# A hybrid decoder layer on one core: output weights of the second token group parted anew by add transfers, and another order of the last half-group

## The chip, the core and the metric

The kernel runs on one core of one Trainium2 chip. The metric is the device time in microseconds of one execution. The kernel before has a median of 1120.68 us over three runs (1118.84 to 1123.88).

## The reference, cut to what matters

One layer of a decoder trunk over 1024 prompt tokens and 64 new tokens (8 sequences of 8), 1024 features, all in float32:

```
h  = rmsnorm(x, norm1_g)
z  = h @ w_in                                    # 1024 -> 2304 columns, for three mixers
ya = gelu(u) * spatial(layernorm(gelu(v)))       # A: gating within chunks of 128 positions, 512 columns
yb = silu(layernorm(conv31(a * sigmoid(g))))     # B: causal depthwise convolution, 256 columns
yc = b * conv3(c * x~)                           # C: short gated convolution, 256 columns
x  = x + concat([ya, yb, yc]) @ w_out            # 1024 -> 1024, the output projection
x  = x + square(relu(rmsnorm(x, norm2_g) @ w_ff1)) @ w_ff2      # 1024 -> 4096 -> 1024
y  = rmsnorm(x, norm_f_g)
```

The outputs are y for both kinds of tokens, the new convolution states and the normalised v rows of the new tokens.

## The kernel before, in words

All 1088 tokens stand on the free axis and features on the 128 partitions, so `x_cm` and `x_cn` hold the features 0 to 511 and 512 to 1023 of the running x, four tiles of 128 features each.

**Products.** TensorE takes each float32 operand as two parts, hi (a copy in fp32r, made by ScalarE) and lo (the difference, made by VectorE). `mm3` issues three matmuls for each pair of tiles: hi by hi (line 174), hi by lo (175 or, by the order of the arguments, 176), lo by hi. Lines 174 to 176 are therefore on nearly all rows of PE, and the names of the operands tell the stage: `yah`, `ybh`, `ych` are the mixers' outputs, `xah`, `xbh`, `xb_yh` and the like operands of the MLP, `wsh`, `wsl`, `wsv`, `wo2l` and some others slots of parted MLP weights.

**Weights up to the output projection.** A list SEQ of 26 weights of 128 x 1024 (0.5 MB) is worked off: 0 to 3 for v, 4 to 17 for the other input columns, 18 to 25 for the eight column blocks `fo` of the output projection. While weight j is in use, `ahead(j)` parts weight j+1 and issues the raw load of j+3. The tiles `raw`, `hi` and `lo` each have a ring of two. During the input projection the parts are made by `split_far` (lines 476 to 485): ScalarE writes lo = -raw (482), GpSimd issues a transfer that loads the weight from HBM once more and adds it onto lo where it was -raw (483), then ScalarE writes hi (484). After the mixers, once the PSUM pool `pairs` is open, parts are made by `split`: hi by ScalarE (167), lo by VectorE (168). At the end of the last input job (its third chunk of tokens, `c == 2` in `in_job`) the next weight is parted already, which is weight 19, the second of the output projection.

**Output projection.** The tokens are in two groups of 544. A product of one `fo` with one group is 8 tiles of features by two pieces of 288 and 256 tokens by three matmuls, 48 matmuls. In the first group three products are begun together without features 4 and 5 (mixer B, which is late; `out_first`), with weight 20 in a pair of tiles of its own, `wo2`; they are finished then, and `out_job` does `fo` 3 to 7. Behind each product VectorE adds x (line 823), ScalarE squares for the norm (825), and VectorE sums the squares (829). Beside that, the weights of the MLP's unit 0 are prepared (`w1_prep`). `out_keep` writes the hi and lo parts of `fo` 0 to 5 to the tensor `wod` in HBM (SP), and `out_fetch` reads them back for the second group. The second group takes the products in the order 6, 7 (whose parts are still in the rings), 0, 1, 2, 3, 4, and 5 in two pieces; `rest` lists what is issued after each; and the norm and parting of the first group's x for the MLP (`x_ops`) are spread over it, three pieces after each product (`some(3)`).

**MLP.** It is 32 units, 0 to 15 for `w_ff1` and 16 to 31 for `w_ff2`, each done by a scheme of seven products in place of eight (steps s = 0 to 6; sums of weight blocks at lines 941 to 945, their parts at 951 and 952, sums of the other operand beside). A step of `w_ff2` accumulates in PSUM: steps 0, 2, 4, 6 in chain 'a', 3 and 5 in chain 'b', 1 in 'c'; after each of them VectorE adds the PSUM to an accumulator (1257). The chain goes on in the same bank, so the next step of a chain can begin only after that. Four pairs of banks are shared out by `ps2`. A table `steps` (1260 to 1262) orders the work; `at(i, job)` puts a job between the matmuls of step i and its evacuation. In units 30 and 31 the tokens are split again into two halves: all steps of both units for the first half, then the same for the second. For the last unit the weight sums and parts are due ten steps before their use (1282), and `g_split` (1217) makes the parts of the MLP's inner activations.

**Final norm.** ScalarE squares and scales x with the gain (`fin_sq`, `fin_scale`), VectorE sums, TensorE takes the mean over the partitions with a matrix of constants (`stat_mm`, 842), VectorE transposes the result (848), computes the inverse root on a few columns (`rstd_newton`) and spreads it by another transpose (152). Then each of eight tiles is multiplied (1329) and sent out (1330). For the first half-group this happens beside the steps of the second one; for the second it is the end of the program (1436 to 1441), on all 544 tokens at once.

## Time and profile before

| | before |
|---|---|
| median of three runs, us | 1120.68 |
| the profiled execution, us | 1121.21 |
| its span, us | 1119.5 |
| mean granted clock of TensorE | 0.971 |
| busy: TensorE, VectorE, ScalarE, GpSimd | 94%, 79%, 37%, 11% |
| transferred, MB | 198.61 |
| mean rate, GB/s | 177 |

The numbers in the tables that follow are from that one execution. A row of the timeline gives start and duration in us, the engine, the line of the kernel, the operation, out<-in, its size, and in brackets how long the engine had been idle and what released it. A row of PE's waits gives the operand, the line and, behind the arrow, what ended the waits; then their total, number and longest. A table by windows gives the window, its length, and for PE, its weight loads, VectorE, ScalarE and GpSimd the busy time with the number of instructions; then the granted clock as a share of the full one, the busy share of the DMA engines, and GB/s. Times on PE of one matmul overlap with the next, so the pace is read from a window's length by its number of matmuls, not from one duration.

### The profile page before, as it was taken

How to read it: one execution, taken by the hardware profiler on the slowest of the kernel's cores; microseconds unless marked ns; L12 is line 12 of the kernel's file. 1: busy time of each engine (PE TensorE's matmuls, PEld its weight loads, DVE VectorE, ACT ScalarE, POOL GpSimd, SP SyncE). 2: the span in 40 equal slices, each digit the busy share in tenths (PEclk: the TensorE clock that was granted, in tenths of full speed). 3: DMA queues.
4: the chain of work that ended last, by engine and by line, in shares of the span. 5: the costliest groups of instructions: out<-in, count | busy, mean ns of one | idle time of the engine just before them, and what ended most of it. 6: DMA issues, size and time to landing. Idle time of an engine off the chain costs nothing.

```text
span 1119.5 us, 19297 instructions
## 1 busy us (share of the span) xinstructions
PE 1048.1 (94%) x7524; PEld 1021.6 (91%) x7524; DVE 879.0 (79%) x1352; ACT 418.4 (37%) x711; POOL 123.5 (11%) x161
## 2 busy tenths in 40 slices
PE   8999999997899789999999999989999999999783
PEld 6789999996889679999999999989999999999773
DVE  6886999964468788778778878886788888888775
ACT  5533455323333333434434344344322222223332
POOL 3751524212000000000000000000000000000030
PEclk8999999998999999999999999999999999999896
DMA  6213454357897355546645645698866766655012
GB/s 222 99 41 73 102 93 80 77 109 209 275 324 238 113 168 184 204 158 215 217 159 194 219 169 181 213 394 289 247 208 216 238 187 227 217 181 194 1 60 101
DMA packets 94219, 198.61 MB, mean 177 GB/s; under 512 B 18288, under 2 KB 24432, under 8 KB 94128
## 3 DMA queue, kind: packets, MB, share of 16 engines
q1 hardware_dynamic: 90240, 183.95, 48.2%
q0 software_dynamic: 3312, 12.32, 6.8%
q8 instruction: 59, 0.97, 0.4%
q10 hardware_dynamic: 576, 1.11, 0.3%
q14 instruction: 32, 0.26, 0.1%
HBM read 129.03 MB, written 68.32 MB: 176 GB/s over the span
## 4 chain that ended last, share of the span: by engine, by line
DVE 38%; PE 35%; DMA 9%; issue 8%; ACT 8%; POOL 1%; SPq 1%; ACTq 0%; DVEq 0%; POOLq 0%
PE pp L174 11%; PE pp L176 11%; PE pp L175 11%; DVE gbuf L571 3%; DVE acc L571 3%; DMA wlo<-in_w 2%; ACT wsh L951 2%; DMA gr<-x_cn 2%; DVE x_cn L1119 1%; DMA gr<-x_cm 1%; DVE x_cn L1118 1%; DVE x_cn L1127 1%; DVE x_cm L1119 1%; DVE x_cm L1118 1%; DVE x_cm L1127 1%
## 5 line engine op out<-in xcount | busy, mean ns | idle before, releaser
L176 PE MATMUL mm<-xh,wlo 128*128 128x384 f32 (+1 forms) x336 | 109.8, 327 | 1.0 <-DMA wlo<-in_w 1.0
L174 PE MATMUL mm<-xh,whi 128*128 128x384 f32 (+1 forms) x336 | 110.2, 328 | 0.0
L175 PE MATMUL mm<-xl,whi 128*128 128x384 f32 (+1 forms) x336 | 109.5, 326 | 0.0
L174 PE MATMUL pp<-xah,wsh 128*128 128x272 f32 x256 | 76.2, 298 | 5.5 <-ACT x_cm L1113 5.0
L176 PE MATMUL pp<-xah,wsh 128*128 128x272 f32 x256 | 74.5, 291 | 0.0
L175 PE MATMUL pp<-xal,wsh 128*128 128x272 f32 x256 | 74.3, 290 | 0.0
L1257 DVE TENSOR_TENSOR x_cn<-pp,x_cn 128x544 f32<-128x544 f32 (+1 forms) x100 | 61.9, 649 | 10.6 <-PE pp L176 10.5
L176 PEld LDWEIGHTS mm<-xh,wlo 128*128 128x128 f32 x336 | 63.1, 188 | 1.6 <-DMA wlo<-in_w 1.6
L174 PE MATMUL pp<-xah,wsl 128*128 128x272 f32 x208 | 61.2, 294 | 2.6 <-ACT x_cm L1113 1.8
L174 PEld LDWEIGHTS mm<-xh,whi 128*128 128x128 f32 x336 | 63.1, 188 | 0.3
L175 PEld LDWEIGHTS mm<-xl,whi 128*128 128x128 f32 x336 | 63.1, 188 | 0.3
L176 PE MATMUL pp<-xah,wsl 128*128 128x272 f32 x208 | 61.1, 294 | 0.0
L175 PE MATMUL pp<-xal,wsl 128*128 128x272 f32 x208 | 60.9, 293 | 0.0
L1257 DVE TENSOR_TENSOR acc_al<-pp,acc_al 128x544 f32<-128x544 f32 (+1 forms) x68 | 44.3, 652 | 20.1 <-PE pp L176 20.0
L1302 POOL DMA_DIRECT2D acc_ah<-x2d x2 | 1.8, 906 | 504.3 <-DMA xbl<-gd 484.1
L174 PEld LDWEIGHTS pp<-xah,wsh 128*128 128x128 f32 x256 | 48.6, 190 | 9.1 <-ACT x_cm L1113 7.1
L951 ACT ACTIVATE wsh<-x_cm 128x512 fp32r<-128x512 f32 x29 | 18.3, 632 | 82.7 <-DVE x_cm L942 82.6
L175 PEld LDWEIGHTS pp<-xal,wsh 128*128 128x128 f32 x256 | 48.8, 191 | 0.0
L176 PEld LDWEIGHTS pp<-xah,wsh 128*128 128x128 f32 x256 | 48.7, 190 | 0.0
L1257 DVE TENSOR_TENSOR acc_ah<-pp,acc_ah 128x544 f32<-128x544 f32 (+1 forms) x68 | 44.2, 650 | 2.7 <-PE pp L176 2.5
L174 PEld LDWEIGHTS pp<-xah,wsl 128*128 128x128 f32 x208 | 40.1, 193 | 3.1 <-ACT x_cm L1113 2.0
L174 PE MATMUL pp<-xbh,wsl 128*128 128x272 f32 x144 | 41.9, 291 | 0.0
(510 smaller groups left out, 3884.4 us busy)
## 6 DMA issues: line engine op xcount, KB each, us to landing
gr<-x_cn SPq DMA_DIRECT2D x64, 272.0 KB, 4.0
wraw<-in_w SPq DMA_DIRECT2D x32, 512.0 KB, 5.0
gr<-x_cm SPq DMA_DIRECT2D x56, 272.0 KB, 5.5
raw<-in_w SPq DMA_DIRECT2D x25, 512.0 KB, 6.8
wlo<-in_w POOLq DMA_DIRECT2D x15, 512.0 KB, 7.4
wrawoh<-in_w SPq DMA_DIRECT2D x15, 512.0 KB, 4.4
wrawol<-in_w SPq DMA_DIRECT2D x15, 512.0 KB, 5.8
xah<-gr SPq DMA_DIRECT2D x26, 272.0 KB, 5.6
```

What stands on the lines that cost most here:

```text
L174: pe.matmul(ps, ah, bh, start=first, stop=False, skip_group_check=chain)
L175: pe.matmul(ps, ah, bl, start=False, stop=False, skip_group_check=chain)
L176: pe.matmul(ps, al, bh, start=False, stop=last, skip_group_check=chain)
L571: dve.scalar_tensor_tensor(out=d, in0=src, scalar=w, in1=d, op0=ALU.mult, op1=ALU.add)
L951: act.activation(out=hi, in_=src, func=AF.Copy)
L1118: dve.tensor_tensor(out=c, in0=c if u == 0 else ps, in1=slot(add, last)[1], op=ALU.add)
L1119: dve.scalar_tensor_tensor(out=c, in0=c, scalar=0.0, in1=c, op0=ALU.max, op1=ALU.mult)
L1127: dve.tensor_tensor(out=c.bitcast(F32R), in0=c, in1=slot(name + "h", True)[1], op=ALU.subtract)
L1257: dve.tensor_tensor(out=a, in0=ps, in1=a, op=ALU.add)
L1302: at(first_use[u + 2 * i, 0] + 1, lambda fo=fos[i]: gp.dma_start(out=acc(fo), in_=x2d[fo], accum_op=ALU.add))
```

## The change

**First group.** The early parting at the end of the last input job now leaves out weight 19 (`nxt[0] < 18`). It is parted in the usual place of the first output job, by which time VectorE makes the lo part and the raw load of weight 21 is issued there too. On ScalarE this moves as follows (first rows of the stretch are mixer B's layer norm and the activation of mixer C; `wlo`, `whi` of the rows with a minus are weight 19, `raw_2120` its raw tile, `wo2h` the hi part of weight 20):

```order
 L736 ACTIVATE gbuf<-gbuf 128x384
 L736 ACTIVATE scr_2305<-acc_1191 128x384
-L482 ACTIVATE wlo_2337<-raw_2120 128x1024
-L484 ACTIVATE whi_2336<-raw_2120 128x1024
-L715 ACTIVATE ych_1674<-scr_2343 128x320
+L715 ACTIVATE ych_1674<-scr_2336 128x320
 L747 ACT_TABLE_LOAD
 L747 ACTIVATE gbuf<-gbuf,parT 128x384
 L747 ACTIVATE acc_1191<-acc_1191,parT 128x384
+L167 ACTIVATE whi_2372<-raw_2120 128x1024
 L167 ACTIVATE wo2h<-raw_2215 128x1024
```

The two copies of the old way stood ahead of the last `ych`; the one copy of the new way stands behind the normalised `gbuf` and `acc`, ahead of weight 20's.

**Second group.** The tensor `wod`, its writes and its reads are gone. For `fo` 3, 0, 1, 2, 4 and 5 `out_load` loads the raw weight again (SP), and `out_parts` parts it as `split_far` does: ScalarE, GpSimd's add transfer, ScalarE. The order of the products becomes 6, 7, 3, 0, 1, 2, 4 and 5 in two pieces, and the loads of MLP unit 0's raw weights (`raw_first`) move from behind the third to behind the fifth product.

**Units 30 and 31, first half.** The preparation of unit 31's seven weight slots is spaced over the ten steps ahead of its first use, and the sums of slot 3 stand one step ahead of its parts. One of the last partings of inner activations is a step later. On VectorE around the evacuation of step 0 of unit 30 (line 1257 before and 1263 after, into `acc_ah` and `acc_al`), the order before is this:

```order
L1257 TENSOR_TENSOR x_cn<-pp_10130,x_cn 128x2x272
L1257 TENSOR_TENSOR x_cn<-pp_10143,x_cn 128x2x272
L952 TENSOR_TENSOR wsv<-wraw_3182,wsv 128x512
L944 TENSOR_TENSOR wrawoh<-x_cm,wrawoh 128x512
L945 TENSOR_TENSOR wrawoh<-wrawoh,x_cm 128x512
L952 TENSOR_TENSOR xbl_3516<-wrawoh,xbl_3516 128x512
L1217 TENSOR_TENSOR xbl_3514<-xbl_3514,xbh_3513 128x1088
L1257 TENSOR_TENSOR acc_ah_7220<-pp_10355,acc_ah_7220 128x272
L1257 TENSOR_TENSOR acc_al_7221<-pp_10362,acc_al_7221 128x272
```

And in the changed kernel, from the same two evacuations of unit 29 on:

```order
L1263 TENSOR_TENSOR x_cn<-pp_10132,x_cn 128x2x272
L1263 TENSOR_TENSOR x_cn<-pp_10145,x_cn 128x2x272
L954 TENSOR_TENSOR wsv<-wraw_3310,wsv 128x512
L1263 TENSOR_TENSOR acc_ah_7222<-pp_10357,acc_ah_7222 128x272
L1263 TENSOR_TENSOR acc_al_7223<-pp_10364,acc_al_7223 128x272
L1222 TENSOR_TENSOR xbl_3516<-xbl_3516,xbh_3515 128x1088
L1263 TENSOR_TENSOR acc_ah_7222<-pp_10375,acc_ah_7222 128x272
L1263 TENSOR_TENSOR acc_al_7223<-pp_10382,acc_al_7223 128x272
L946 TENSOR_TENSOR wrawoh<-x_cm,wrawoh 128x512
L947 TENSOR_TENSOR wrawoh<-wrawoh,x_cm 128x512
```

Ahead of the evacuation of step 0 stood four preparations, two of them sums, and a parting of 1088 columns; now one preparation stands there, and the others follow between the evacuations.

**Second half.** The steps of units 30 and 31 are done in the order 0, 1, 2, 4, 6 for each unit, and then 3, 5 for each; chain 'b' takes the pair of banks `q`. The final norm's sums on VectorE stand behind the evacuation of their step instead of ahead of it (`then`). On PE around the statistic of the first half's norm (line 842), with `xb_yl` and `wsh` the operands of step 2, the order before is this:

```order
L174 MATMUL pp_10601<-xb_yl,wsh_3429 128x272
L175 MATMUL pp_10601<-xb_yl,wsh_3429 128x272
L176 MATMUL pp_10601<-xb_yl,wsh_3429 128x272
L842 MATMUL pp_10646<-xb_yh,means 128x288 x2
L842 MATMUL pp_10646<-xb_yh,means 128x256 x2
L174 MATMUL pp_10661<-xah_2942,wsl_3430 128x272
L175 MATMUL pp_10661<-xal_2943,wsl_3430 128x272
L176 MATMUL pp_10661<-xah_2942,wsl_3430 128x272
```

And in the changed kernel:

```order
L174 MATMUL pp_10603<-xb_yl,wsh_3431 128x272
L175 MATMUL pp_10603<-xb_yl,wsh_3431 128x272
L176 MATMUL pp_10603<-xb_yl,wsh_3431 128x272
L842 MATMUL pp_10652<-xb_yh,means 128x288 x2
L842 MATMUL pp_10652<-xb_yh,means 128x256 x2
L174 MATMUL pp_10596<-xb_yl,wsh_3510 128x272
L175 MATMUL pp_10596<-xb_yl,wsh_3510 128x272
L176 MATMUL pp_10596<-xb_yl,wsh_3510 128x272
```

Behind the statistic stood step 3, in a bank of its own (`pp_10661`); now step 4 stands there, which goes on in the chain that step 2 was in.

**Final norm.** Steps 0, 1 and 6 add to the first 272 tokens of a half-group, steps 2 to 5 to the other 272, and with the new order the first are complete four steps before the end. `early` norms tokens 0 to 255 of the last half-group there, the inverse root on GpSimd, three output products on VectorE and five on GpSimd. The tail then works on the other 288 tokens: part of the sum of squares is left to TensorE, which accumulates several tiles in one statistic (`stat_tok`); then come the chain of the inverse root, eight products of 288 tokens on VectorE, and the outputs.

The diff, cut:

```diff
-                if c == 2:
+                if c == 2 and nxt[0] < 18:
                     ahead_of(nxt[0])
...
-        for i in range(2):
-            if fo < 6:
-                sp.dma_start(out=wod[fo, i], in_=f(wt[i]))
...
-    def out_fetch(fo, tags=None):
...
+    def out_load(fo):
+        wor[fo] = ring.tile([P, 1024], F32, tag="raw", name=nm("wor"))
+        sp.dma_start(out=wor[fo], in_=w[18 + fo])
+
+    def out_parts(fo, tags=("hi", "lo")):
         wob[fo] = [ring.tile([P, 1024], F32R, tag=t, name=nm("wob")) for t in tags] if tags else wo2
-        for i in range(2):
-            sp.dma_start(out=f(wob[fo][i]), in_=wod[fo, i])
+        hi, lo = wob[fo]
+        raw = wor.pop(fo)
+        act.activation(out=lo, in_=raw, func=AF.Copy, scale=-1.0)
+        gp.dma_start(out=lo, in_=w[18 + fo], accum_op=ALU.add)
+        act.activation(out=hi, in_=raw, func=AF.Copy)
...
+            if fo == 5:
+                out_load(3)
             if fo == 6:
-                out_fetch(0, ("raw", "raw"))
+                out_parts(3, None)
+                out_load(0)
+            if fo == 7:
+                out_load(1)
...
+            i = q if g0 and name == "b" else (2 * (u % 2) + TAGS[name] + q) % 4
...
-    steps += [(u, s, (g,)) for g in range(2) for u in (UNITS - 2, UNITS - 1) for s in range(7)]
+    steps += [(u, s, (0,)) for u in (UNITS - 2, UNITS - 1) for s in range(7)]
+
+    steps += [(u, s, (1,)) for u in (UNITS - 2, UNITS - 1) for s in (0, 1, 2, 4, 6)]
+    steps += [(u, s, (1,)) for u in (UNITS - 2, UNITS - 1) for s in (3, 5)]
...
-                i = max(last_use[UNITS - 3, (2, 2, 3, 3, 4, 4, 5)[s]] + 1, first_use[u, s] - 10)
+                i = max(last_use[UNITS - 3, (2, 2, 3, 3, 4, 4, 5)[s]] + 1, first_use[u, 0] + (-10, -9, -8, -4, -3, -2, -1)[s])
...
+            elif u == UNITS - 1 and s == 3:
+                at(when[u, s] - 1, lambda u=u, s=s: w_sums(s, wraw[u % 2], stemp[0]))
+                at(when[u, s], lambda u=u, s=s: w_parts(s, wraw[u % 2], stemp[0], last_slot(s)))
...
+    def fin_sqs(i, g, fos, cut=(0, G2), half=None):
+
+        def sums():
+            for fo, sc in zip(fos, scs):
+                fin_add(g, fo, sc, cut)
+            if half:
+                fin_half(g, half)
+
+        scs = []
+        at(i, lambda: scs.extend(fin_sq(g, fo, cut) for fo in fos))
+        at(i, lambda: [fin_scale(g, fo, cut) for fo in fos])
+        then(i, sums)
...
+    CUT = [(0, 256), (256, 288)]
+    for i, fos in [(-8, (0, 1)), (-7, (4, 5)), (-1, (2, 3)), (0, (6, 7))]:
+        fin_sqs(E[0] + i, 0, fos, half=(0, G2) if i == 0 else None)
+    for i, fos, t in [(2, (0, 1), 0), (5, (4, 5), 0), (7, (2, 3), 0), (10, (6, 7), 0), (11, (4, 5), 1), (12, (0, 1), 1)]:
+        fin_sqs(E[0] + i, 1, fos, TH[t])
...
+    def stat_chain(g, ps, cut):
+        t = (G2 * g + cut[0], cut[1])
+        sc = fin[0][:, t[0]:t[0] + t[1]]
+        dve.transpose(out=sc, in_=ps[:, :cut[1]])
+        rstd_newton(t, sc)
+        rstd_bcast(t, sc)
...
+    def early():
+        ps = pair(2)
+        t = (G2, CUT[0][1])
+        sc = fin[0][:, t[0]:t[0] + t[1]]
+        stat_tok(ps, [sc], mean1k_f)
+
+        def pow_():
+            dve.transpose(out=sc, in_=ps[:, :t[1]])
+            rstd_pow(t, sc)
+
+        def outs():
+            rstd_bcast(t, sc)
+            for i, fo in enumerate((2, 0, 1, 4, 3, 6, 5, 7)):
+                fin_out(1, fo, gp if i % 2 == 0 or i > 5 else dve, sp, CUT[0])
+        then(E[0] + 11, pow_)
+        then(E[0] + 13, outs)
+
+    at(E[0] + 11, early)
+    last_sq = {}
+    at(E[0] + 13, lambda: last_sq.update({fo: fin_sq(1, fo, TH[1]) for fo in (6, 7)}))
+    at(E[0] + 13, lambda: [fin_scale(1, fo, TH[1]) for fo in (6, 7)])
...
         else:
             for q in range(2):
                 ff2_out(u, s, q, gr)
+        for job_ in after.pop(i, []):
+            job_()
...
-    rest = [lambda: out_fetch(1, ("hi", "lo")), lambda: out_fetch(2, ("hi", "lo")), raw_first,
-            lambda: out_fetch(4, ("hi", "lo")), lambda: out_fetch(5, ("hi", "lo")), lambda: None, slot_ring]
+    rest = [lambda: (out_parts(0), out_load(2)),
+            lambda: (out_parts(1), out_load(4)),
+            lambda: (out_parts(2, None), out_load(5)),
+            lambda: out_parts(4),
+            lambda: (out_parts(5), raw_first()),
+            lambda: None, slot_ring]
     stemp[0] = vv[0][:, 0:512]
     norm_half(0)
-    for i, fo in enumerate((6, 7, 0, 1, 2, 3, 4)):
+    for i, fo in enumerate((6, 7, 3, 0, 1, 2, 4)):
...
-    fin_sqs(1, (6, 7), (0, H))
-    ps = pair(0)
-    stat_mm([fin[0][:, gs(1)]], ps, (0, G2), mean1k_f)
-    stat_rest(1, ps, fin[0], (0, G2))
-    for i, fo in enumerate((0, 1, 4, 5, 2, 3, 6, 7)):
-        fin_out(1, fo, dve, act if i % 2 else sp)
+    ps = pair(3)
+    o = G2 + CUT[1][0]
+    stat_tok(ps, [fin[0][:, o:o + 288]], mean1k_f, last=False)
+    for fo in (6, 7, 2, 3):
+        sq = last_sq[fo] if fo in last_sq else fin_sq(1, fo, TH[1])
+        stat_tok(ps, [sq], mean1k_f, 16, False, fo == 3)
+    stat_chain(1, ps, CUT[1])
+    for fo in (2, 3):
+        fin_scale(1, fo, TH[1])
+    for i, fo in enumerate((0, 1, 4, 5, 6, 7, 2, 3)):
+        fin_out(1, fo, dve, act if i % 2 else sp, CUT[1])
```

45 lines of the change are left out of this document (21 added, 24 removed).

## The prediction

> **What bounds the kernel now.** I read the page first, then PE's waits, then the busy time of four stages, then single rows of the timeline. The page:
>
> ```profile
> PE 1048.1 (94%) x7524; PEld 1021.6 (91%) x7524; DVE 879.0 (79%) x1352; ACT 418.4 (37%) x711; POOL 123.5 (11%) x161
> ```
>
> PE is the bound, so the change can only win where PE waits or runs at a lowered clock, or in the tail after its last matmul. PE's waits, longest in total first (total, times, longest):
>
> ```profile
> PE pp L174 <- DVE acc_ah L1257: 8.5, 5, 3.4
> PE pp L176 <- DMA wlo<-in_w: 7.2, 1, 7.2
> ...
> PE pp L176 <- DVE wlo L168: 3.3, 4, 1.0
> ...
> PE pp L174 <- ACT whi L167: 2.2, 3, 1.2
> ```
>
> All four lie in stages that the change touches. The stages (us; PE, PEld, DVE, ACT, POOL busy; granted clock, DMA share, GB/s), and one undisturbed stretch for comparison:
>
> ```profile
> 254.69:324.85 70.16, 57.53 (x392) 55.17 (x393) 32.19 (x50) 23.14 (x36) 5.76 (x5) 0.88 0.82 269
> 324.85:373.60 48.75, 48.75 (x389) 48.75 (x387) 38.70 (x59) 18.02 (x24) 0.00 (x0) 1.00 0.68 233
> 1040.42:1070.90 30.48, 24.87 (x173) 24.27 (x172) 22.52 (x44) 11.17 (x18) 0.00 (x0) 0.89 0.01 1
> 1070.90:1119.50 48.60, 26.12 (x175) 24.06 (x173) 30.99 (x65) 15.04 (x29) 12.02 (x8) 0.79 0.25 92
> ...
> 980.00:1000.00 20.00, 20.00 (x161) 20.00 (x160) 16.78 (x26) 6.32 (x9) 0.00 (x0) 1.00 0.43 137
> ```
>
> Row one is the output projection of the first token group: 70.2 us. Row two is the same eight products for the second group, PE busy throughout: 48.75 us, or 6.1 a product. So the first group loses about 20 us to waits and to a clock of 0.88. The last row gives 20/161 = 0.124 us a matmul, 1.5 us for a step of 12. The last two units (30 and 31) are 28 such steps, 42 us, but stretch from 1040.42 to 1100.3; then comes a tail of 19.2 us to 1119.5.
>
> **A. First group of the output projection.** Its second product waits for a lo part made by an add transfer, and then runs at half clock:
>
> ```profile
> 268.07 0.61 PE L176 MATMUL pp<-yah,wlo 128*128 128x288 f32 x1 [7.21 <-DMA wlo<-in_w]
> 268.47 0.45 PE L174 MATMUL pp<-yah,whi 128*128 128x288 f32 x1
> ...
> 255.00 0.94 POOL L483 DMA_DIRECT2D wlo<-in_w  x1 [0.82 <-ACT wlo L482]
> ```
>
> The transfer is issued at 255.00 and landed 13.0 us later (the largest of its kind, row below). The edit at line 527 takes this one lo part away from the add path: the weight is split after the pairs pool opens, hi on ACT, lo on DVE. When is that ready? In before the neighbours are:
>
> ```profile
> 258.27 0.69 ACT L747 ACTIVATE acc<-acc,parT 128x384 f32<-128x384 f32 x1
> 258.87 1.04 ACT L167 ACTIVATE wo2h<-raw 128x1024 fp32r<-128x1024 f32 x1
> ...
> 259.94 1.23 DVE L168 TENSOR_TENSOR wo2l<-raw,wo2h 128x1024 fp32r<-128x1024 f32 x1 [1.46 <-ACT acc L747]
> ```
>
> ACT loses the two copies that stood before the last ych (about 0.9 us of delay for it), and gains one copy between the first of these rows and the second: hi from about 258.0 to 259.05, lo on DVE to 260.35. PE wants it at 260.8 (268.07 less 7.21). The stall of 7.2 goes, and with it some 2.5 us of half clock (23 matmuls at 0.24 instead of 0.13 us). What is late next: the layer norm on DVE is about 1 us later by the added 1.2 us, and the PE statistic of its third chunk waits perhaps 0.4 us. The third weight is covered, its product starting 5 us later.
>
> The moved step has a transfer too, the raw load of the fourth weight. On SP it stood ahead of the x2 loads, and now stands behind them:
>
> ```profile
> 255.68 0.34 SPq L161 DMA_DIRECT2D raw<-in_w  x1
> 262.22 2.63 SPq L796 DMA_DIRECT2D x_cm<-in_x  x4
> ```
>
> It goes out at 264.9 instead of 255.7 and, with the 7.5 us of the row on landings below, is there at 272.4; its split can start at 271.5, when the first of three held products frees a slot, and its product at 274.6. So it costs 0, with 2.2 us of cover less the 2.3 of the split.
>
> The rest of the loss is waits for hi and lo parts (2.2 + 3.3 us) and the half clock after them (the remainder, about 5 us). The writes to `wod` hold the ring slots that the next split needs:
>
> ```profile
> 297.53 1.06 ACT L167 ACTIVATE whi<-raw 128x1024 fp32r<-128x1024 f32 x1 [4.02 <-DMA wod<-whi]
> ```
>
> With them gone a slot is free at the end of its product, and split takes 1.06 + 1.23 us of a 6.1 us product. Two waits stay: the product after the held ones (its split stands behind three evacuations on DVE; 0.8), and one behind the load of x2 for features 512 and up (0.6). A: 20.3 lost now, 1.8 then: 18.5 gained. Bounds: 12 (only the 7.2, its clock and half of the rest) to 20.
>
> **B. Second group.** Six weights are loaded raw and parted anew: per weight two ACT copies (1.06 + 1.04) and one add transfer issued by POOL. PE is full here, so nothing can be won; what can be lost is an add that lands too late. Of the fifteen in before:
>
> ```profile
> L483 POOL DMA_DIRECT2D wlo<-in_w x15: 857/877/1079, 80.9 to 255.0; - x15
> ...
> DMA to landing us min/median/max: 6.2/7.5/13.0
> ...
> 335.17 0.66 ACT L825 ACTIVATE rb<-x_cn 128x544 f32<-128x544 f32 x1 [2.46 <-DVE x_cn L823]
> ```
>
> Except for weight 3, the copies are queued on ACT behind the square of the product that frees the slot, and the product that needs them begins two products (12.2 us) later. The square of product 0 ends at 335.8, 4.9 us after that product (324.85 + 6.1); the lo copy adds 1.06, the transfer 7.5: 13.5, so 1.3 us late. The product served this way frees a slot in its turn, late by as much, and the one served from there adds its own 1.3: about 3 us of PE in all. It is hidden by DVE, which ends the stage:
>
> ```profile
> 367.62 0.30 PE L174 MATMUL pp<-yah,wob 128*128 128x288 f32 x1
> ...
> 371.11 0.72 DVE L823 TENSOR_TENSOR x_cn<-pp,x_cn 128x544 f32<-128x544 f32 x1
> ```
>
> DVE evacuates product 6 at 371.11, 3.5 us after PE has left it. So PE may be 3 us late unseen, and what counts is DVE: ACT's copies delay an `x_hi`, for which DVE waits about 0.7 us, and the two raw tiles of unit 0 arrive later (0.3). I take 1 us lost. Bounds 0 and 6 (adds landing in 10 us).
>
> One rule speaks against this part. The Trainium skill, SBUF — State Buffer, "SBUF: two separate sides", says that a transfer issued by GpSimd starves for its descriptors while VectorE holds their shared port. Here:
>
> ```profile
> 140.00:160.00 20.00, 20.00 (x124) 20.00 (x123) 20.00 (x26) 10.96 (x24) 6.26 (x12) 1.00 0.50 75
> ```
>
> DVE was busy all of these 20 us, and of all fifteen issues none took over 1.08 us. The trace so far does not bear the rule out for these DVE operations; its result is the third rival.
>
> **C. First half of units 30 and 31.** In before DVE prepares unit 31 (line 1282, ten steps ahead) in front of evacuations that PE waits for:
>
> ```profile
> 1043.83 0.36 PE L174 MATMUL pp<-xah,wo2l 128*128 128x272 f32 x1 [1.74 <-DVE x_cn L1257]
> ...
> 1049.00 0.56 PE L174 MATMUL pp<-xb_yl,wsh 128*128 128x272 f32 x1 [3.42 <-DVE acc_ah L1257]
> ...
> 1042.96 1.35 DVE L1257 TENSOR_TENSOR x_cn<-pp,x_cn 128x544 f32<-128x544 f32 x2
> ...
> 1048.42 0.43 DVE L1257 TENSOR_TENSOR acc_ah<-pp,acc_ah 128x272 f32<-128x272 f32 x1
> ...
> 1070.53 0.29 PE L174 MATMUL pp<-xb_yh,wo2h 128*128 128x272 f32 x1
> ```
>
> Fourteen steps take 30.1 us instead of 21. The first wait (1.9 from the end of step 0) stays, since nothing ahead of 1044.2 on DVE moves. Then DVE now does one part (0.6) and evacuates step 0 at 1044.8 instead of 1048.4, and PE starts step 2 on it almost without a wait. The parts and sums follow singly between evacuations of 0.7: 1.2 to 1.9 us of DVE a step against PE's 1.5, so I count three more waits of 0.3 to 0.4. Sum 3 us lost instead of 9; 6 gained. Bounds 3.5 (half clock once, from the 1.9 us gap) and 8.
>
> **D. Last half-group on PE.** The new order runs the accumulating steps 2, 4 and 6 of a unit one after another on one bank. The norm of the first half-group stands on DVE ahead of the evacuation of step 2:
>
> ```profile
> 1077.97 0.75 DVE L848 STREAM_TRANSPOSE fin<-pp 128x544 f32<-128x544 f32 x1 [1.31 <-PE pp L842]
> ...
> 1080.89 0.40 DVE L1257 TENSOR_TENSOR acc_ah<-pp,acc_ah 128x272 f32<-128x272 f32 x1
> ```
>
> In before PE had step 3, on another bank, to do in those 2.9 us; now it has nothing, and stands about 3.4 us, after a wait of 1.0 for the halves. So this is a wait that the change adds: 4.5 us. It removes the others (the pair at 1091 among them). 14 steps 21, waits 4.5, two statistics 1.1: 26.6. Add half clock after such a gap, priced by
>
> ```profile
> 1091.01 0.39 PE L174 MATMUL pp<-xb_yl,xbh 128*128 128x272 f32 x1 [1.82 <-DVE acc_ah L1257]
> ...
> 1092.78 0.43 PE L174 MATMUL pp<-xah,xbl 128*128 128x272 f32 x1
> ```
>
> where 1.8 us of idle time was followed by 18 matmuls spaced 0.23 instead of 0.12 us: 2.0. That makes 28.6 against 29.8 in before (1070.5 to 1100.3): 1.2 gained, bounds 3 gained to 3 lost. The Trainium skill, TensorE: Matmul & The Clock Gate, "The HAM clock gate", halves the clock only after about 3.4 us without work; by that my gap lies on the border, and the sum would be 2 us less if it stays below.
>
> **E. The tail.**
>
> ```profile
> 1100.02 0.29 PE L176 MATMUL pp<-xbh,xbh 128*128 128x272 f32 x1
> ...
> 1106.77 0.75 DVE L848 STREAM_TRANSPOSE fin<-pp 128x544 f32<-128x544 f32 x1 [2.34 <-PE pp L842]
> ...
> 1109.83 0.73 DVE L1329 TENSOR_TENSOR acc_ah<-acc_ah,fin 128x544 f32<-128x544 f32 x1
> ...
> 1113.65 1.35 DVE L1329 TENSOR_TENSOR x_cn<-x_cn,fin 128x544 f32<-128x544 f32 x2
> ...
> 377.46 0.48 DVE L848 STREAM_TRANSPOSE rb<-pp 128x288 f32<-128x288 f32 x1 [0.16 <-PE pp L842]
> ...
> 379.32 0.48 DVE L152 STREAM_TRANSPOSE rb<-rcmp 128x288 f32<-128x288 f32 x1
> ```
>
> Now: 6.5 us from the last matmul to the transpose, 3.1 to the first product, 5.2 for eight products of 544, 4.5 to the end. Then: 256 tokens are finished in the shadow of the last steps (three products on DVE, five on POOL). For the other 288: two squares on ACT and their matmuls, 2.0 to the transpose; the chain by the two rows of 288 columns, 2.3; eight products at 5.2/8 x 288/544 = 0.34 and a little for their start, 3.0; 4.0 to the end, taking 0.5 off for the smaller transfers. 11.3 instead of 19.2: 8 gained. POOL's products may slow DVE's, as in before (0.78 to 1.2 us); bounds 5 and 9.
>
> **The sum**, against the profiled execution, 1121.2 us (span 1119.5 and 1.7 around it): 18.5 - 1 + 6 + 1.2 + 8 = 32.7, so 1088.5. The median shown, 1120.7, is 0.5 below that execution, so I forecast 1088.
>
> **Rivals.**
> 1. *The adds land like the one at 255.00.* With 13 us instead of 7.5 the lateness by the rule of rival 3 is 2 x 5.3 less 3, with half clock after two gaps (2.0 each): 12 us lost. For it: DMA share 0.68 in this stage already, and 0.82 where the 13.0 fell. Against: the median of 7.5. Time 1100.
> 2. *The first group gets back only the stall.* If raw loads or x2 loads, not `wod` writes, hold the splits, A is 10 and not 18.5: 1097. Against: the row at 297.53 names the write.
> 3. *Slower: starved adds.* Every add stretched by DVE, which is busy 38.70 of 48.75 us there, so that PE runs the second group at the pace of the transfers. The loss is about twice (landing + 4.5 - 12.2) less 3 hidden; 4.5 stands for the way from a product's end to the end of the lo copy once DVE is no longer behind. To eat 32.7 and 5.6 more it must be 41, a landing of 28 us: twice the longest seen. At 30 us the time is 1130.
> 4. *It does not do what it says:* adds and copies cost in the second group what the first wins; 18.5 lost in B leaves the end's 15: 1106, still faster.
>
> **How the numbers follow.** About 0.5%, 5.6 us, is what a measurement of this kernel tells from no change. Forecast 0.74; rival 1 0.10; rival 2 0.07; rival 4 0.03; rival 3 0.03; 0.03 that several shortfalls together leave no gain to measure. Best ends of A to E: 20, 0, 8, 3, 9, together 40: 1081. All worst ends together are unlikely; their deviations (6.5, 5, 2.5, 4, 3) added as squares give 10: 1098, and rival 1 stretches it to 1100. Faster by over 0.5%: 0.94; within: 0.03; slower: 0.03.
>
> **What would show it.** In the changed profile: no wait of PE on a DMA for wlo, and the first group in some 52 us at a clock near 1 (A); PE waits of 1 to 3 us on DMA wob or wo2l in the second group, and no later start of the next stage relative to its end (B); steps 2 and 3 of unit 30 without a 3.4 us gap (C); a new gap of 3 to 4 us behind L842 in unit 30's second half (D); 11 to 12 us from the last step to the end (E). I am wrong if the adds land in over 10 us or if the first group keeps its waits.

## The result, and the profile after

The changed kernel takes 1095.32 us (median of four runs, 1094.60 to 1096.16), the kernel before 1122.28 us in the runs beside them (four, 1118.84 to 1125.10). The ratio is 0.9761, with a 95% interval from 0.9730 to 0.9793: 27 us faster. A second measurement of both kernels (f1 below) gives a ratio of 0.9788, 25 us. The forecast was 1088, between 1081 and 1100. So sign, size and range held, and some 6 to 8 of the 33 us that were expected are missing.

The profiled execution took 1094.89 us, its span 1093.2, 26.3 less than before. The line of the page on the engines:

```profile
PE 1042.3 (95%) x7532; PEld 1017.2 (93%) x7532; DVE 879.3 (80%) x1359; ACT 430.9 (39%) x734; POOL 132.7 (12%) x173
```

The work on each engine is nearly what it was. What went is time in which TensorE waited or ran slowly. The windows by stage (first group; second group; first half of units 30 and 31; last half-group; tail; columns as in the prediction):

```profile
254.27:305.63 51.36, 50.44 (x390) 49.39 (x391) 33.42 (x51) 22.82 (x35) 4.82 (x4) 1.00 0.63 211
305.63:357.90 52.27, 49.89 (x390) 49.09 (x388) 39.74 (x61) 29.31 (x36) 5.24 (x6) 1.00 0.84 242
1025.70:1049.64 23.94, 21.97 (x170) 21.38 (x169) 20.71 (x43) 10.71 (x18) 0.00 (x0) 1.00 0.01 2
1049.64:1080.70 31.06, 25.26 (x176) 24.32 (x174) 23.04 (x51) 15.36 (x36) 13.04 (x10) 0.89 0.19 73
1080.70:1093.20 12.50, 2.62 (x12) 1.82 (x10) 8.46 (x21) 2.19 (x6) 3.99 (x5) 0.82 0.56 178
```

The first group runs at a clock of 1.00 where it ran at 0.88. The last half-group does not: 0.89 in 31.06 us. The table below counts each stage from the first matmul of the stage to the first of the next one, for all profiled executions of this study; the tail starts at the end of the last step's matmuls. (The prediction's 70.2 counts to the edge of its window.) The two rows of changes are taken from unrounded figures.

| execution | first group | second group, to the first MLP step | MLP to unit 30 | units 30, 31, first half | last half-group | tail |
|---|---|---|---|---|---|---|
| before | 70.0 | 52.6 | 663.2 | 30.1 | 29.8 | 19.2 |
| changed | 51.4 | 55.1 | 665.0 | 23.9 | 31.2 | 12.3 |
| forecast: change in us | -18.5 | +1 | 0 | -6 | -1.2 | -8 |
| measured: change in us | -18.7 | +2.5 | +1.8 | -6.2 | +1.4 | -6.9 |
| e1_late_split | 62.4 | 52.7 | 665.9 | 29.0 | 29.8 | 19.0 |
| e2_add_transfers | 57.5 | 56.0 | 664.2 | 30.1 | 29.8 | 18.7 |
| e3_end_only | 70.2 | 52.7 | 665.8 | 24.0 | 31.2 | 12.2 |
| e4_spaced_preps | 67.1 | 52.6 | 664.8 | 25.2 | 29.8 | 18.6 |
| e5_copies_first | 51.3 | 61.2 | 664.7 | 23.9 | 31.2 | 12.3 |
| e6_interleaved_end | 51.3 | 56.4 | 663.2 | 23.9 | 29.1 | 13.3 |
| e7_both | 51.3 | 60.9 | 664.8 | 24.0 | 29.0 | 13.3 |
| e8_parts_by_vector | 51.4 | 62.9 | 665.8 | 24.0 | 31.2 | 12.3 |
| f1_changed_again | 51.3 | 55.1 | 664.4 | 24.0 | 31.2 | 12.3 |
| f2_second_group | 51.3 | 53.9 | 664.6 | 23.9 | 31.2 | 12.3 |
| f3_second_half | 51.3 | 54.8 | 665.0 | 24.0 | 25.7 | 13.8 |
| f4_both | 51.4 | 53.9 | 665.0 | 24.0 | 25.7 | 13.8 |

With the changed code the last three stages agree within 0.2 us from one execution to the next. Others differ more with the same code: the first group of the kernel before (67.1 to 70.2 us), the changed second group (54.8 to 56.4), the MLP (663.2 to 665.9), and, with the code before, the first half of units 30 and 31 (29.0 to 30.1) and the tail (18.6 to 19.2). The profile before is at the long end of the last two. So of the measured 6.2 and 6.9 us, up to 1.1 and 0.6 can be the luck of that execution.

PE's waits after, those of the stages that the change touches:

```profile
PE pp L174 <- DVE acc_ah L1263: 4.3, 2, 3.4
PE pp L176 <- DMA wob<-in_w: 2.3, 2, 1.3
PE pp L842 <- ACT yah L108: 2.2, 1, 2.2
...
PE pp L842 <- DVE acc_ah L1263: 1.5, 1, 1.5
...
PE pp L176 <- DVE wlo L168: 0.9, 2, 0.7
```

The wait of 7.2 us on `wlo` is gone, the waits for `whi` too, and 0.9 us is left of those for the lo parts by VectorE. New are two waits on the adds (`wob`), and 1.5 and 3.4 us around the statistic of the first final norm.

Second group. The adds' landing times (issues by queue, number, size, median us from issue to landing), and where ScalarE and VectorE stood:

```profile
wob<-in_w POOLq DMA_DIRECT2D x4, 512.0 KB, 7.3
...
wo2l<-in_w POOLq DMA_DIRECT2D x2, 512.0 KB, 8.0
```

```profile
306.72 1.06 ACT L926 ACTIVATE wo2l<-wor 128x1024 fp32r<-128x1024 f32 x1 [3.08 <-DMA wor<-in_w]
...
309.30 0.73 DVE L829 TENSOR_TENSOR rb<-rb 128x544 f32<-128x544 f32 x1 [2.74 <-ACT rb L825]
...
320.64 1.29 DVE L888 TENSOR_TENSOR xal<-x_cm,xah 128x1088 fp32r<-128x1088 f32 x1 [1.02 <-ACT xah L884]
...
351.88 0.69 DVE L943 TENSOR_TENSOR wraw<-wraw,wraw 128x512 f32<-128x512 f32 x1 [1.12 <-DMA wraw<-in_w]
```

The adds land as forecast. The time is lost on VectorE. ScalarE stands 3 us for a raw load with the last square of the first group behind it; its copies then delay an `x_hi`; and unit 0's raw weights are late. VectorE evacuates product 6 of the group 48.9 us after the group's start, against 46.4 before (371.11 less 324.7).

Last half-group. TensorE, VectorE and GpSimd at the first norm and behind it:

```profile
1055.86 0.73 PE L842 MATMUL pp<-xb_yh,means 128*128 128x288 f32 x4 [1.53 <-DVE acc_ah L1263]
1059.97 0.59 PE L174 MATMUL pp<-xb_yl,wsh 128*128 128x272 f32 x1 [3.39 <-DVE acc_ah L1263]
...
1065.20 0.29 PE L174 MATMUL pp<-xb_yh,xah 128*128 128x272 f32 x1
```

```profile
1067.27 2.38 DVE L1338 TENSOR_TENSOR fin<-fin,x_cm 128x272 f32<-128x272 f32 x2
1069.58 0.43 DVE L1263 TENSOR_TENSOR acc_ah<-pp,acc_ah 128x272 f32<-128x272 f32 x1
```

```profile
1065.15 5.70 POOL L1351 TENSOR_TENSOR x_cn<-x_cn,fin 128x544 f32<-128x544 f32 x4
```

```profile
1070.76 0.39 PE L174 MATMUL pp<-xb_yl,xah 128*128 128x272 f32 x1 [0.88 <-DVE acc_ah L1263]
```

Two steps behind the 3.39 us run at 0.23 us a matmul in place of 0.125, up to 1064.7; two windows show how the granted clock went:

```profile
1054.49:1057.91 3.42, 0.73 (x4) 0.55 (x4) 2.38 (x6) 1.94 (x6) 0.00 (x0) 1.00 0.00 0
1057.91:1061.32 3.41, 1.35 (x6) 1.35 (x7) 3.27 (x8) 0.00 (x0) 1.59 (x2) 0.50 0.00 0
```

Then a third wait follows, of 0.88 us, which the prediction did not have. VectorE has two additions ahead of the evacuation, 2.38 us together, while GpSimd multiplies; the same addition takes 0.43 us when GpSimd rests (at 1077.61).

Tail. VectorE between the last evacuation and the end:

```profile
1082.11 1.81 DVE L1351 TENSOR_TENSOR x_cn<-x_cn,fin 128x256 f32<-128x256 f32 x2
1083.84 0.47 DVE L1391 STREAM_TRANSPOSE fin<-pp 128x288 f32<-128x288 f32 x1
...
1086.65 0.46 DVE L1351 TENSOR_TENSOR acc_ah<-acc_ah,fin 128x288 f32<-128x288 f32 x1
```

The transpose that opens the last chain stands behind two of the early products, 0.9 us each. It could not have begun much sooner: the matmuls of the statistic that it reads end at 1083.3, 0.5 us before it.

### The profile page after: what moved, and what is told of

It reads as the page before. It is cut to its first block, busy times and chain, and to the rows that moved or that the text cites. A ratio compares the mean times of both kernels' runs of the same rounds, so it can differ in the third digit from the quotient of the medians.

```text
span 1093.2 us, 19347 instructions
## 1 busy us (share of the span) xinstructions
PE 1042.3 (95%) x7532; PEld 1017.2 (93%) x7532; DVE 879.3 (80%) x1359; ACT 430.9 (39%) x734; POOL 132.7 (12%) x173
## 4 chain that ended last, share of the span: by engine, by line
PE 36%; DVE 36%; DMA 9%; ACT 9%; issue 8%; POOL 1%; SPq 1%; ACTq 0%; DVEq 0%; POOLq 0%
PE pp L174 12%; PE pp L176 11%; PE pp L175 11%; DVE gbuf L571 3%; DVE acc L571 3%; DMA gr<-x_cn 2%; ACT wsh L953 2%; DVE x_cn L1132 1%; DMA wlo<-in_w 1%; DVE x_cn L1124 1%; DMA gr<-x_cm 1%; DVE x_cn L1123 1%; DVE x_cm L1123 1%; DVE x_cm L1124 1%; DVE x_cm L1132 1%
## 5 line engine op out<-in xcount | busy, mean ns | idle before, releaser
L174 PE MATMUL pp<-xah,wsl 128*128 128x272 f32 x208 | 60.9, 293 | 1.9 <-ACT x_cm L1118 1.8
```

Source lines behind the costliest of these rows:

```text
L174: pe.matmul(ps, ah, bh, start=first, stop=False, skip_group_check=chain)
```

## The experiments

The theory that the prediction left, as it stood after the result: the gains lie in three places that add up. In the first group they come from the stall at line 527 and, apart from it, from the writes to `wod`; in the first half of units 30 and 31 from the order on VectorE; at the end from the shorter tail. The losses are on VectorE's and ScalarE's order, not in the adds. The chief rivals: the stall alone explains the first group; the adds themselves, or the DMA load, explain the second.

### Parts of the change alone (before as the base)

**e1_late_split**: line 527 only.

```diff
-                if c == 2:
+                if c == 2 and nxt[0] < 18:
```

> The kernel before with the edit at line 527 alone: weight 19 is parted behind the mixers, by VectorE; the writes to wod and the reads stay. My theory: the stall of 7.2 us and its half clock (2.5) go, and the waits that the writes to wod cause stay, so the first group takes about 60 us instead of 70.2 and the time is about 10 us below the kernel before (1112). Rival: the whole of the 18.8 us that the first group won comes from this one stall and what followed it, and the writes to wod held nothing: 1103.5, first group 51 to 52 us. At either time I expect no wait of PE on a DMA for wlo in that group, and a second group of 49 us as before.

Measured: 1114.83 us against 1119.66, ratio 0.9953 (0.9936 to 0.9969), 5 us faster. The first group takes 62.4 us: 7.6 won. PE's waits there, and the window:

```profile
PE pp L174 <- ACT whi L167: 3.7, 2, 2.1
PE pp L176 <- DVE wlo L168: 2.9, 4, 0.9
```

```profile
254.68:317.09 62.41, 55.76 (x390) 53.83 (x391) 33.26 (x51) 23.14 (x35) 4.82 (x4) 0.92 0.84 303
```

The stall is gone, and 6.6 us of waits for hi and lo parts stay, at a clock of 0.92. So the rival falls: the stall is less than half of the gain. (The time gains less than the stage, because the MLP of this execution took 2.8 us longer.) What the parts wait for is seen on ScalarE:

```profile
288.19 1.06 ACT L167 ACTIVATE whi<-raw 128x1024 fp32r<-128x1024 f32 x1 [4.46 <-DMA wod<-whi]
```

This copy and the next two start within 0.1 us of the landing of a write to `wod` (288.11, 297.51 and 307.07), while the raw weights that they read had landed 9 to 11 us earlier (279.30, 286.82 and 296.26, counted by the order of the loads). So the raw loads do not hold these parts.

**e2_add_transfers**: `wod` replaced by raw loads and add transfers, with the new order of products; line 527 and the end as before.

```diff
-                sp.dma_start(out=wod[fo, i], in_=f(wt[i]))
...
+        act.activation(out=lo, in_=raw, func=AF.Copy, scale=-1.0)
+        gp.dma_start(out=lo, in_=w[18 + fo], accum_op=ALU.add)
+        act.activation(out=hi, in_=raw, func=AF.Copy)
```

> The kernel before with the output weights of the second group loaded and parted anew by add transfers, no wod, and nothing else (line 527 as before). My theory: the stall of 7 us on wlo at the second product stays, the waits for hi and lo parts in the rest of the first group go (8 to 9 us won), and the second group and the way to the first MLP step lose 2.65 us as in the changed kernel: about 6 us faster, 1116. Rival (all of the first group's gain is the stall at line 527): nothing won in the first group, 2.65 lost in the second, 1125.

Measured: 1112.69 us, ratio 0.9942 (0.9922 to 0.9962), 6.5 us faster. PE's waits of the first group and both windows:

```profile
PE pp L176 <- DMA wlo<-in_w: 4.6, 1, 4.6
...
PE pp L176 <- DVE wlo L168: 0.9, 2, 0.7
```

```profile
253.22:310.76 57.54, 52.05 (x390) 50.77 (x391) 32.39 (x50) 22.83 (x36) 5.76 (x5) 0.97 0.63 195
310.76:366.77 56.01, 50.75 (x392) 49.69 (x391) 41.44 (x64) 30.29 (x39) 5.24 (x6) 0.99 0.80 230
```

The first group wins 12.5 us although the stall stays (4.6 us here; 4.9 and 4.7 in the next two runs, which have the old code there, and 7.2 in the profile before: the prediction read an uncommonly late transfer). The waits for `whi` are gone. So it is the writes to `wod`, which hold the slots of the rings, that made them. Part of the 12.5 is the shorter stall; without a stall on either side, from e1 to the changed kernel, the same edit wins 11.0. It also takes away the first reads of `wod` and their traffic, which was not tried apart from the writes; the rows of ScalarE in e1 name the writes. The two edits win 7.6 and 12.5 alone and 18.7 together.

**e3_end_only**: units 30 and 31 and the final norm as in the changed kernel, the output projection as before.

```diff
+    steps += [(u, s, (1,)) for u in (UNITS - 2, UNITS - 1) for s in (0, 1, 2, 4, 6)]
+    steps += [(u, s, (1,)) for u in (UNITS - 2, UNITS - 1) for s in (3, 5)]
...
+    fin_out(1, fo, dve, act if i % 2 else sp, CUT[1])
```

> The kernel before with only the edits to units 30 and 31 and to the final norm; output projection as before. My theory, that the parts add up: first half of units 30 and 31 6.2 won, second half 1.3 lost, tail 6.7 won, so 11.6 us faster, 1110.7. If the tail or the first half owe their gain to a kernel that arrives there with another clock or other loads, it is less: the rival gives 6 or less, 1116. The order of the accumulating steps should again show two waits of some 1.5 and 3.4 us around the first norm's statistic.

Measured: 1109.89 us, ratio 0.9910 (0.9892 to 0.9929), 10 us faster. By stages 6.1 won, 1.4 lost, 7.0 won, as in the changed kernel; the MLP of this execution took 665.8 us. So these three stages owe their change to nothing that comes before them.

**e4_spaced_preps**: only the spacing of unit 31's preparation, with one parting a step later.

```diff
-                i = max(last_use[UNITS - 3, (2, 2, 3, 3, 4, 4, 5)[s]] + 1, first_use[u, s] - 10)
+                i = max(last_use[UNITS - 3, (2, 2, 3, 3, 4, 4, 5)[s]] + 1, first_use[u, 0] + (-10, -9, -8, -4, -3, -2, -1)[s])
```

> The kernel before with only the preparation of unit 31 spaced out (and one parting a step later); steps of the second half, final sums and tail as before. My theory: the preparations in front of the evacuations are what PE waits for in the first half of units 30 and 31, so this alone wins about 6 us, 1116.3, and the 3.4 us gap ahead of step 2 of unit 30 is gone. Rival: the final norm's sums that stand ahead of the evacuations of unit 31 (deferred only in the full change) hold PE as much: 3 to 4 us won, 1118.5.

Measured: 1114.24 us, ratio 0.9956 (0.9939 to 0.9972), 5 us faster. The first half of the two units takes 25.2 us, 4.9 less than in the profile before (3.8 less than in e1, the shortest with the code before). Its waits on VectorE:

```profile
PE pp L174 <- DVE x_cn L1257: 1.7, 1, 1.7
PE pp L174 <- DVE acc_ah L1257: 0.9, 1, 0.9
```

The 3.4 us gap is gone. The 0.9 us that is left here is missing in the full change. It stands at step 2 of unit 31, where the final norm's sums were not yet put behind the evacuation. So 4.9 of 6.2 us are the spacing; the rest goes with the deferred sums, which was read from where the wait stands and not tried alone.

### The losses

e5 to e8 ran on another chip than the other experiments; the kernel before took 1119.28 us there. They are compared with the first measurement of the changed kernel, 1095.3 us.

**e5_copies_first**: the copies and adds of the second group ahead of the norm and the evacuation, and two raw loads ahead of x loads on SP.

```diff
+                out_load(3)
+                x2_fill(1, 1)
...
+        if i < 5:
+            rest[i]()
         if i == 0:
             norm_stat(0, new_pair(), rb2)
```

> The changed kernel, with the copies and add transfers of the second group issued right behind the product that frees the slot, ahead of the norm statistic, the evacuation and the square, and with the raw loads of weights 3 and 0 ahead of the x loads on SP. My theory for the 2.65 us that the second group lost: ScalarE stood 3 us waiting for a raw load with the square of product 7 behind it, its copies delayed an x_hi by 1 us, and unit 0's raw weights came 1.1 us late. All three go: second group to first MLP step 52.4 to 53 us instead of 55.06, and no wait of PE on DMA wob; 2 to 2.6 us faster than the changed kernel (1092.9). Rival: the loss is the transfers' own (DMA engines busy 0.84 of the stage), which the same transfers in another order do not cure: 1095.3, waits on wob as before.

Measured: 1100.53 us, ratio 0.9827 (0.9808 to 0.9846), 5 us slower than the changed kernel. The theory failed in this form. ScalarE, and the waits of PE in the stage:

```profile
315.63 1.06 ACT L926 ACTIVATE wob<-wor 128x1024 fp32r<-128x1024 f32 x1 [6.19 <-DMA wor<-in_w]
```

```profile
PE pp L176 <- DMA wob<-in_w: 4.8, 3, 2.4
PE pp L842 <- ACT yah L108: 2.4, 1, 2.4
PE pp L176 <- DMA wo2l<-in_w: 1.6, 1, 1.6
```

The raw load of weight 0 went out earlier and took 10 us, beside four x loads, and now the root of the norm stood behind ScalarE's wait for it, 6.2 us; the stage is 6.1 longer than in the changed kernel. Counted from the start of the group, the load went out 3.7 us earlier and landed 2.5 us earlier. An order that waits for a load is only as good as the load.

**f2_second_group**: three smaller moves, with the changed kernel beside it (f1 below); the hi copy of weight 0 is now issued behind `some(3)`.

```diff
+            if fo == 5:
+                out_load(3)
             if fo in (5, 6):
                 x2_fill(6 - fo, 1)
...
+        last = lambda: act.activation(out=hi, in_=raw, func=AF.Copy)
+        return last if fo == 0 else last()
...
         out_evac(fo, 1, ps, i == 0)()
+        if i == 6:
+            w_sums(2, wraw[0], stemp[0])
+            w_sums(3, wraw[0], stemp[0])
```

> The changed kernel with three small moves in the second group, one for each loss read from its trace: the raw load of weight 3 goes ahead of x loads on SP (0.35 us: ScalarE then does not stand with the square of product 7 behind it), the hi copy of weight 0 behind the first two x_hi (1.0), and unit 0's sums of raw weights behind the last whole evacuation (1.1). Theory: the stage goes from 55.06 to 52.6 us and the kernel by 2 to 2.5 us. Rival, after the run in which all copies went ahead: what sets this stage is when raw loads and adds land, and these moves only shift waits: 55 us, and waits of PE on wob of 1 us and more as before.

Measured: 1092.55 us, ratio 0.9752 (0.9733 to 0.9770); the stage takes 53.9 us in place of 55.1.

```profile
PE pp L176 <- DMA wob<-in_w: 1.7, 3, 1.1
PE pp L842 <- ACT yah L108: 1.4, 1, 1.4
```

By the stage, 1.2 of the 2.5 us come back (53.9 in f4 too, outside the 54.8 to 56.4 of the unaltered stage), between theory and rival: the waits for the adds stay. In the trace two of the three losses are gone, at the transpose and at the raw weights; VectorE still waits 0.9 us for the first `x_hi`, behind a lo copy whose raw load lands late. The medians of f2 and f1 are 2.9 us apart; what is over 1.2 stands in no stage that f2 touches.

**e8_parts_by_vector**: the lo parts of the second group by VectorE.

```diff
-        act.activation(out=lo, in_=raw, func=AF.Copy, scale=-1.0)
-        gp.dma_start(out=lo, in_=w[18 + fo], accum_op=ALU.add)
         act.activation(out=hi, in_=raw, func=AF.Copy)
+        dve.tensor_tensor(out=lo, in0=raw, in1=f(hi), op=ALU.subtract)
```

> The changed kernel, with the lo parts of the second group's six weights made by VectorE (raw less hi) and not by add transfers. My theory: VectorE ends the second group, so six subtractions of 1.23 us on it cost about 7 us, less what the six lo copies on ScalarE and the waits on wob gave: 4 to 7 us slower than the changed kernel (1101). Rival: VectorE has slack there (busy 39.7 of 52.3 us), the adds' waits and the delayed squares weigh as much, and the two are equal within 1 us: 1095.3.

Measured: 1103.73 us, ratio 0.9857 (0.9838 to 0.9876), 8 us slower than the changed kernel; the stage takes 62.9 us. What TensorE then waits for:

```profile
PE pp L842 <- ACT yah L108: 9.2, 2, 8.9
```

VectorE ends this stage, and work that is put on it lengthens it: six subtractions of 1.23 us are 7.4, measured 7.8. That is just over the 4 to 7 expected: the six lo copies that ScalarE no longer makes gave nothing back.

**e6_interleaved_end**: the steps of the two units in turn, so that no step follows one of its own chain; the norm's root on GpSimd.

```diff
+    X, Y = UNITS - 2, UNITS - 1
+    steps += [(u, s, (1,)) for u, s in ((X, 0), (X, 1), (Y, 0), (X, 2), (Y, 2), (X, 4), (Y, 4), (X, 6), (Y, 6), (Y, 1),
+                                        (X, 3), (Y, 3), (X, 5), (Y, 5))]
...
+    at(E[0] + 3, first_stat)
+    then(E[0] + 3, first_pow)
+    then(E[0] + 5, lambda: rstd_bcast((0, G2), fin[0][:, 0:G2]))
```

> The changed kernel, with the steps of units 30 and 31 interleaved in the last half-group so that two steps of one chain never follow each other (the two halves of a step share a pair of banks for that), the statistic of the first norm one step later, its inverse root on GpSimd and its transposes behind the evacuations. My theory: the second half is long because of waits of PE for the evacuation of the step before (1.5, 3.4, 0.9) and the half clock behind them (2.2), so it comes down from 31.2 us to 23 to 25, and the time by 6 to 8: 1088. Rival: VectorE, busy 23 of these 31 us, becomes the bound and the waits come back elsewhere: 28 us, 1092.

Measured: 1092.80 us, ratio 0.9763 (0.9744 to 0.9782): 2 us less for the half-group, 1 more for the tail, no difference that the times show. The rival, nearly to the number (29 us). Twelve steps run without a wait of more than 0.5 us; then TensorE stands at the early norm for sums that VectorE has not done:

```profile
1072.26 0.67 PE L1409 MATMUL pp<-fin,means 128*128 128x256 f32 x2 [3.69 <-DVE fin L1348]
```

```profile
1064.81 2.71 DVE L1348 TENSOR_TENSOR fin<-fin,x_cm 128x272 f32<-128x272 f32 x2
```

But VectorE was not full with work: its additions took 1.36 us each and not 0.43.

**e7_both**: the edits of e5 and e6.

> The changed kernel with the edits of the two runs before together (copies first in the second group, interleaved steps at the end). If the stages are independent: the sum of both, some 9 us below the changed kernel, 1086. If a stage that begins earlier or with another clock gives part of it back: the larger of the two alone, 1088 to 1090.

Measured: 1099.50 us, ratio 0.9820 (0.9801 to 0.9839). By stages it is e5 in the second group and e6 in the half-group; the stages are independent, and one of the two edits is bad.

**f1_changed_again**: the changed kernel.

> The changed kernel itself, unaltered, on the chip and in the rounds of the three runs beside it. Expected: 1095.3 as before, first group 51.4, second group to first MLP step 55.1, last half-group 31.2, tail 12.3. It also tells how far stages that nothing touches (the MLP's 663 to 666 us) differ from one execution to the next.

Measured: 1095.41 us, ratio 0.9788 (0.9767 to 0.9808), with the same stages within 0.1 us but for the MLP (664.4).

**f3_second_half**: e6, with the squares of four tiles given to TensorE for the early norm and left to VectorE only for the 16 columns that the last chain needs.

```diff
-    stat_tok(ps, [sc], mean1k_f)
+    stat_tok(ps, [sc] + [a[:, :256] for a in esq], mean1k_f)
...
+            for sc in scs:
+                s = slice(G2 + 256, G2 + H)
+                dve.tensor_tensor(out=fin[0][:, s], in0=fin[0][:, s], in1=sc[:, 256:H], op=ALU.add)
```

> The changed kernel with interleaved steps in the last half-group as before, and four of the sums of squares for the early norm taken from VectorE and given to TensorE, because VectorE's additions took 1.2 to 1.4 us instead of 0.43 each while GpSimd multiplied, and TensorE stood 3.7 us for them. Theory: TensorE no longer waits at the early norm, keeps its clock, and the half-group takes 24 to 26 us (31.2 in the changed kernel, 29.05 with the steps alone interleaved); the tail 12.5 to 13.3; 5 to 6 us faster than the changed kernel. Rival: VectorE is full all the same and the tail waits for it: half-group 25, tail 16, at most 2 us faster.

Measured: 1089.16 us, ratio 0.9725 (0.9706 to 0.9743), 6 us faster than the changed kernel beside it. The half-group takes 25.7 us; its window runs at a clock of 1.00, and these are all of its waits:

```profile
1048.43:1073.93 25.50, 24.50 (x185) 23.47 (x183) 20.27 (x43) 14.05 (x33) 12.91 (x10) 1.00 0.17 67
```

```profile
PE pp L174 <- DVE acc_al L1272: 0.5, 1, 0.5
PE pp L174 <- DVE x_cn L1272: 0.4, 1, 0.4
```

**f4_both**: f2 and f3.

> The edits of the second group and of the last half-group together. If the stages are independent: 8 us below the changed kernel, 1087. If the rivals of both hold: 1093 or more.

Measured: 1089.12 us, ratio 0.9722 (0.9703 to 0.9741). The stages are those of f2 and f3: 1.2 us less in the second group, 5.5 less in the half-group, 1.5 more in the tail. In time it does not differ from f3 alone; either is about 0.6% below the changed kernel, and both beat the two kernels that were compared.

## Why the prediction held, point by point

**What bounds the kernel.** That TensorE sets the time and only its waits, its clock and the tail can give anything held in every run.

**A, first group: right, 18.5 against 18.7.** e1 and e2 show both causes that the sum named. Within it two sizes were off and made up for each other, so that the closeness of the total is in part luck. The stall with its clock was put at 9.7 and brought 7.6 in e1, where the other waits grew from 5.4 to 6.6 us once it was gone; from e2 to the changed kernel, with the writes gone already and a shorter stall, it brought 6.2. The rest, the writes to `wod`, was put at 8.8 and is worth 11.0 with the stall gone, with the half clock that follows short waits. The stall is also commonly nearer 5 than the 7.2 us of that one profile: that rows of one execution carry a transfer's luck was not allowed for. Rival 2 (only the stall) is excluded by e1.

**B, second group: right in the mechanism, 1 against 2.5.** The adds landed in 7.3 and 8.0 us (medians), where 7.5 was reckoned (the landings 6.2/7.5/13.0 count the writes from `wlo` to `wod` too; the fifteen adds alone have 6.8/7.4/13.0), and PE was late by 1.35 and 0.93 where 1.3 was reckoned; rival 1 is out. VectorE was the end of the stage, as said (e8). The terms that were too small are the two on the other engines: for the delayed `x_hi` 0.7 was put and 1.0 measured, and for the raw weights of unit 0, 0.3 was put and 1.1 measured. Not seen was the wait of ScalarE for a raw load ahead of a square (0.2 us at the transpose). f2 got half of the 2.5 back.

The rule of the Trainium skill (SBUF — State Buffer, "SBUF: two separate sides") that the third rival took up, transfers issued by GpSimd starving while VectorE holds the port, did not show: VectorE was busy 39.74 of 52.27 us in this stage, and the adds landed as fast as in before. The section tells it of VectorE's two-port modes, such as an fp32 copy; VectorE's work in this stage is nearly all additions, subtractions and multiply-adds, so such copies were not put to the test.

**The MLP, not in the sum, +1.8.** Its own steps were not changed. It takes 663.2 to 665.9 us in the fourteen executions; the profile before was at the low end. A good part of the difference is the clock at the start of unit 0. In the clock records of these traces every stretch at half clock, but the one that the end of a run cuts off, is 3.41 us long or a multiple of it, so the clock is set anew on a grid of 3.41 us. Two such windows of the kernel before, and two of the changed kernel, around the wait ahead of unit 0:

```profile
372.17:375.58 3.41, 1.67 (x14) 1.47 (x13) 2.39 (x5) 1.90 (x4) 0.00 (x0) 1.00 0.22 82
375.58:379.00 3.42, 2.37 (x16) 2.17 (x17) 2.30 (x8) 1.08 (x3) 0.00 (x0) 1.00 0.25 81
```

```profile
358.18:361.59 3.41, 1.53 (x10) 1.32 (x11) 2.08 (x6) 1.30 (x3) 0.00 (x0) 1.00 0.13 44
361.59:365.00 3.41, 3.41 (x18) 3.41 (x17) 2.35 (x9) 1.60 (x5) 0.00 (x0) 0.50 0.11 38
```

In the changed kernel 1.8 of the 2.2 us of waiting fall into one window; TensorE is busy 1.53 of its 3.41 us, and the next window has half the clock: its matmuls start 0.23 us apart in place of 0.125, which loses about 1.5 us. In the kernel before, the wait at the same place was longer, 2.7 us, but the border at 375.58 parts it into 1.74 and 0.95, TensorE is busy 1.67 of 3.41 us, and the clock stays. Over all windows of the fourteen traces, those at full clock with TensorE busy under 0.44 of the time were always followed by half the clock, those over 0.56 never, and in between both occur. So the length of one wait does not tell whether the clock falls; the busy share of a window does, and where the grid lies differs from one execution to the next. This also goes with the spread of the MLP: the two shortest executions (before and e6) spend 10.2 us of it at half clock, the three longest (665.8 to 665.9) 19.7 to 22.6, though between these the order is not strict.

**C: right, 6 against 6.2** (5.1 against e1's 29.0), and by the reason given (e4), with a part that the deferred sums brought.

**D, last half-group: wrong in sign, 1.2 gained forecast, 1.4 lost.** The step of the prediction that the new order puts a wait behind the statistic held: 1.53 and 3.39 us, reckoned as 1.0 and 3.4, and the half clock 2.2 against 2.0 (the stretch at 1092 that priced it has some 15 slow matmuls and not 18, 1.6 us). What failed is "it removes the others": a third wait of 0.9 us came. Of the 2.6 us that the forecast was off, 0.5 are in the first of these waits and 0.9 in the third; the rest is in small pieces, matmuls that start farther apart behind each wait, and the two matmuls of the early norm's statistic, which hold up the steps by some 0.5 us at 1077. The sign was there in the kernel before: its wait of 1.82 us at 1091 stands behind an addition of VectorE that took 1.68 us beside GpSimd's products, where the same addition takes 0.73 us without them (at 1099.26). e6 and f3 show what stood behind it. With the chains interleaved the waits for evacuations go, and what is left is VectorE's additions beside GpSimd; with those taken away the half-group needs 25.7 us, 5.5 less.

The other rule that the prediction weighed (the Trainium skill, TensorE: Matmul & The Clock Gate, "The HAM clock gate") would have left the clock up below about 3.4 us of idleness. Here the clock fell within the gap of 3.39 us, at 1057.91, when TensorE had stood for only 1.3 us: the window from 1054.49, with most of the wait of 1.53 us in it too, had 0.73 us of work. The 2.2 us of unit 0 also speak against 3.4 us as a threshold for one wait.

**E, tail: right in the mechanism, 8 against 6.9.** The eight products took 3.0 us, as reckoned. The way to the transpose took 3.0 and not 2.0, of which the ten matmuls of the statistic, in a row from 1080.74 to 1083.3, are 2.5 and the early products on VectorE the last 0.5. The chain then took 2.8 and not 2.3, and the end 3.5 and not 4.0. The prediction named GpSimd's hold on VectorE in its bounds but not in its value (its 0.78 looks like a row of two evacuations, which were not slowed; additions were, 1.18 and 1.68 in place of 0.73).

The sum: 0.41 (the projection began earlier) + 18.66 - 2.51 - 1.85 + 6.16 - 1.43 + 6.86 = 26.3, the difference of the spans.

## What to carry to other kernels

A tile that is written to HBM to be read later holds its ring slot until the write has ended; where the next part is made in that slot, the writes can set the pace; here they cost 11 us of TensorE's time. Rows of one execution carry luck: a stall of 7.2 us in one profile was 4.6 to 4.9 in three others, and a stage with a clock that falls can differ by 1 us or more, so read a second profile before a term goes into a sum. Interleave two chains that accumulate in banks of their own, so that an evacuation always has a step to hide behind, and move additions to an engine that has room before giving multiplications to GpSimd beside a VectorE that works from SBUF. Where an engine works in order, a copy that waits for a load goes behind the work that others wait for.
